# Rearranging the end of the second mixer, and the last token tile's output, in a two-layer trunk kernel

## The chip, the cores and the metric

The kernel runs as one program on one core of a Trainium2 chip. The metric is device time in microseconds. The core has a matmul engine (PE in the profile, with its weight loads shown apart as PEld), three engines that work on tiles (DVE, the vector engine; ACT, the scalar engine; POOL), and queues that issue DMA transfers (most of them from SP). Each engine works through its own list of instructions in order; semaphores make one engine wait for another. Matmul results go to PSUM, of which this program uses eight banks of 128 x 512 floats; everything else lies in SBUF.

## What is computed

The reference is a two-layer encoder over 512 tokens of width 1024. Layer A mixes with a matrix memory, layer B with banded attention; both also attend to 256 memory tokens, and each mixer is followed by a gated MLP with a short convolution. The part that the change touches is layer B's mixer and the final norm:

```python
h = rmsnorm(x, norm_mix_g[l])
proj = h @ b_w_in[bl]
q, q_mem = jnp.split(proj, [B_WIDTH], axis=-1)
mix_out = band_attention(q, k_pad, v_pad, b_rel_bias[bl])      # 12 heads of 64
w_out = b_w_out[bl]
mem_out = memory_attention(q_mem, mem, mem_w_kv[l])            # 4 heads of 64, 256 keys
x = x + jnp.concatenate([mix_out, mem_out], axis=-1) @ w_out
x = x + conv_ffn(rmsnorm(x, norm_ffn_g[l]), ffn_w_up[l], ffn_conv_w[l], ffn_conv_b[l], ffn_w_down[l])
...
return rmsnorm(x, final_g)
```

`k_pad` and `v_pad` are shared keys and values, projected from the normed output of layer A with `w_kv`.

## The kernel before

Activations are kept feature-major: eight tiles of 128 features by 512 tokens. Every matmul operand is split into a high part and a low part in a reduced float type (`split`, L139: the high part is a cast on ACT, L140, the low part a subtraction on DVE, L141). A product is then three matmuls: high by high, high by low, low by high (`mm3`, L192; the PE rows of L194, L195 and L196). A weight tile that arrives by DMA as `wr` becomes `wh` and `wl` in the same way; there are three buffers of `wr` and three of each part.

**Pairs.** Heads are worked on two at a time. The 12 band heads are six pairs, 0 to 5, and the four memory heads are two pairs, 0 and 1. `project_pair(j)` (L1309) makes values, keys and queries of band pair j: three projections of 24 matmuls each, the values transposed (L1323), the queries formed by `queries` and `head_queries` (two casts at L525 and two at L528 on ACT, two subtractions at L526 on DVE, two memsets on POOL at L524). `b_memory_queries(hp)` (L1391) is one projection of 24 matmuls and the same forming of queries. A projection's result is scaled on DVE at L574 (queries) or L1312 (values and keys); only when that has run does its PSUM bank come free.

**Attention.** `memory_attention` (L582) has, for each of two halves of the tokens and each head: scores on PE (L544), a maximum on DVE (L598), the exponential on ACT (L601, twice), a reciprocal (L602) and a scaling (L604, twice) on DVE, four transposes on PE (L613), and a split of the transposed tile (`pt`; ACT L140, DVE L141). Two groups of four matmuls (L627), one for each head, then multiply by the values; `values` (L559) adds their halves (ACT L563, DVE L564). `band_attention` (L1333) does the same by four token tiles T = 0 to 3 of growing width: scores (L544), bias and minimum on DVE (L1350), exponential on ACT (L1354), reciprocal and scaling on DVE (L1355, L1356), transposes (L1365), split, and the products with the values (L1386, L1387).

**PSUM.** The eight banks form three rings: three banks for projections (`mm`, shown as `pmm`), three for scores (`sc`, `psc`), two for transposes and value products (`tr`, `ptr`). A new tile of a ring waits until the last reader of the tile that used the bank before has finished.

**Order.** In this stage nothing is ordered by hand, except that a few instructions are pinned. The code is written as generators that yield after each small piece of PE work. `weave(job, filler, each, lead)` (L225) runs an attention as `job` and takes `each` pieces of the filler for every piece of the job; `chain` puts generators one after another; `until` runs the filler until a result is there; `run` runs it to its end. The filler holds work that depends on little: the remaining projections, then the output projection (`OutProjection.part(g, *ks)`, which loads rows k of `b_w_out` and adds their product into the open sums of output group g). A scheduler of the language then lists the instructions engine by engine, by readiness as it reckons it, so the engines' lists follow the written order only roughly. `reload_x` (L437) issues eight loads on SP that bring the residual back into the buffers `fh` and `fl`, which until then hold the values of band pairs 1 to 4.

**The end.** After the last MLP the output is token-major: four tiles T of 128 tokens, each in two halves of 512 features (`xt[T][0]` and `xt[T][1]`). `add_squares` (L1434) collects sums of squares in pieces, and `final_norm` (L1445) forms the reciprocal root (a square root on ACT, a reciprocal and one Newton step on DVE), scales one half on ACT and the other on DVE, and sends both out by DMA, one from ACT's queue and one from SP's.

Of the kernel before, what the change touches and what calls it, by code (L numbers as in the profile page):

```python
# [12 lines left out]
AF = mybir.ActivationFunctionType  # L13
# [3 lines left out]
P = 128  # L17
D = 1024
# [36 lines left out]
def trunk(  # L55
# [526 lines left out]
    def memory_attention(q, kv, hp, mixes):  # L582
# [40 lines left out]
        for h in range(2):  # L623
            o2 = ps("tr")
            outs.append(o2)
            for i, (a, p) in enumerate(((0, pth), (0, ptl), (1, pth), (1, ptl))):
                nc.tensor.matmul(o2, vs[a][:, 2 * hp + h, :], p[h][:, a, :], start=i == 0, stop=i == 3)  # L627
            yield
# [767 lines left out]
    fill = chain(*(project_pair(j) for j in range(5)), b_memory_queries(0), project_pair(5), b_memory_queries(1))  # L1396
# [7 lines left out]
    until(lambda: 4 in qkv, fill)  # L1404
    weave(band_attention(4, *qkv.pop(4)), fill, 3.456)
    run(fill)
    reload_x()
    fill = chain(outp.part(0, 0, 1), outp.part(0, 2, 6), outp.part(0, 3, 4))
    weave(memory_attention(memq[1], memkv, 1, mixes), fill, 0.48, 4)
    job = band_attention(5, *qkv.pop(5))  # L1410
    fill = chain(fill, outp.part(0, 7))
    weave(islice(job, 8), fill, 2.372)
# [21 lines left out]
    def add_squares(T, t):  # L1434

        if len(sums[T]) == 1:
            V.tensor_scalar(sums[T][0], sums[T][0], 1.0 / D, EPS, op0=ALU.mult, op1=ALU.add)
        elif sums[T]:
            last = sums[T].pop()
            V.scalar_tensor_tensor(sums[T][0], last, 1.0 / D, sums[T][0], op0=ALU.mult, op1=ALU.add)  # L1440
        sums[T].append(small(1))
        sq = sb("t", [P, S])
        A.activation(sq[:, : t.shape[-1]], t, AF.Square, accum_out=sums[T][-1])

    def final_norm(T):  # L1445
        v, r, t = small(1), small(1), small(1)
        first, second = sums[T]
        A.activation(r, second, AF.Sqrt, scale=1.0 / D, bias=first)
        V.scalar_tensor_tensor(v, second, 1.0 / D, first, op0=ALU.mult, op1=ALU.add)
        V.reciprocal(r, r)  # L1450
        V.tensor_mul(t, r, r)
        V.scalar_tensor_tensor(t, t, -0.5, v, op0=ALU.mult, op1=ALU.mult)
        V.scalar_tensor_tensor(r, t, 1.5, r, op0=ALU.add, op1=ALU.mult)
        A.activation(xt[T][0], xt[T][0], AF.Copy, scale=r)
        nc.scalar.dma_start(out[T * P : (T + 1) * P, :S], xt[T][0])
        V.scalar_tensor_tensor(xt[T][1], xt[T][1], r, fgb[1], op0=ALU.mult, op1=ALU.mult)
        nc.sync.dma_start(out[T * P : (T + 1) * P, S:], xt[T][1])
# [80 lines left out]
```

## Time and profile before

| what | value |
|---|---|
| time, median of 3 runs | 1179.51 us (1179.32 to 1180.14) |
| the profiled execution's own time | 1181.13 us |
| its span, first to last instruction | 1179.4 us |
| PE busy over the span | 1167.9 us (99%) |
| DVE, ACT, POOL busy | 941.3, 730.0, 129.7 us |
| mean granted clock of PE | 0.999 |
| second mixer's memory pair 0, first scores to band pair 4 | about 743 to 755 us of the span |
| its end, products of band pair 5 | about 802 us |
| last matmul of the program | issued at 1172.11 us |

The profile gives for each instruction its engine, source line, tiles and shape, its start from the beginning of the span, its duration, and, in brackets, how long the engine had been idle and which instruction released it. Durations of one engine can overlap: matmuls of the same kind follow each other at a shorter distance than each lasts, so for what a matmul costs the distance between starts counts. A line with `x4` is four equal instructions merged. "The windows" are a view that gives, for stretches of the span, how long each engine was busy in them.

### The profile page before, as it was taken

Reading aid. Unit: us, or ns where it says so; the run is one execution under the profiler, and the core shown is the slowest. Engines: PE = TensorE matmul, PEld = TensorE weight load, DVE = VectorE, ACT = ScalarE, POOL = GpSimd, SP = SyncE. Lnnn points to the kernel's source line nnn. Section 1 sums busy time; section 2 is a strip of 40 time slices with the busy share of each in tenths; the row PEclk is TensorE's granted clock in tenths of the full one; section 3 lists DMA queues with packets and bytes.
Section 4 is the critical chain, followed back from the end, with each engine's and each line's share of the span. In section 5 each row is a group of like instructions: output and inputs, shape, how many; then the busy total and the mean of one; then the engine's idle time right before and its main releaser. Section 6 shows DMA issues by size and latency. Waiting matters only on the chain.

```text
span 1179.4 us, 18657 instructions
## 1 busy us (share of the span) xinstructions
PE 1167.9 (99%) x7007; PEld 1033.9 (88%) x7007; DVE 941.3 (80%) x1688; ACT 730.0 (62%) x1294; POOL 129.7 (11%) x222
## 2 busy tenths in 40 slices
PE   8999999999999999999999999999999999999997
PEld 8988888888889999999888888888889999999986
DVE  5877778787979877777697888897897887777755
ACT  5638578654656665556576667776565665666545
POOL 0211101000011111111021000101001011110100
PEclk9999999999999999999999999999999999999999
DMA  8645425244366866666564312335426466566551
GB/s 283 206 116 132 105 54 152 66 136 134 90 155 146 189 157 171 151 154 136 146 196 134 90 54 80 105 104 179 143 90 152 109 137 143 142 143 143 126 161 72
DMA packets 200156, 158.64 MB, mean 135 GB/s; under 512 B 8344, under 2 KB 179838, under 8 KB 200066
## 3 DMA queue, kind: packets, MB, share of 16 engines
q1 hardware_dynamic: 183906, 119.74, 34.7%
q0 software_dynamic: 15584, 36.67, 15.7%
q8 instruction: 55, 0.90, 0.3%
q10 hardware_dynamic: 576, 1.05, 0.2%
q14 instruction: 35, 0.29, 0.1%
HBM read 128.89 MB, written 32.46 MB: 137 GB/s over the span
## 4 chain that ended last, share of the span: by engine, by line
PE 93%; DVE 3%; DMA 2%; ACT 1%; SPq 1%; issue 0%; POOL 0%; POOLq 0%; ACTq 0%; DVEq 0%
PE pmm L194 18%; PE pmm L195 18%; PE pmm L196 18%; PE ptr L195 6%; PE ptr L194 6%; PE ptr L196 6%; PE psc L196 5%; PE psc L195 5%; PE psc L194 5%; PE psc L544 2%; PE ptr L1365 1%; DMA wr<-in_mem_w_kv_dram 1%; PE ptr L1386 1%; PE ptr L1387 1%; DMA u<-in_mem_dram 1%; PE ptr L627 1%
## 5 line engine op out<-in xcount | busy, mean ns | idle before, releaser
L194 PE MATMUL pmm<-u,wh 128*128 128x512 f32 (+1 forms) x968 | 333.0, 344 | 0.2 <-ACT u L140 0.2
L196 PE MATMUL pmm<-u,wl 128*128 128x512 f32 (+1 forms) x968 | 330.7, 342 | 0.0
L195 PE MATMUL pmm<-u,wh 128*128 128x512 f32 (+1 forms) x968 | 330.4, 342 | 0.0
L141 DVE TENSOR_TENSOR wl<-wr,wh 128x1024 fp32r<-128x1024 f32 (+3 forms) x172 | 199.9, 1163 | 81.6 <-ACT wh L140 81.2
L140 ACT CAST wh<-wr 128x1024 fp32r<-128x1024 f32 (+3 forms) x172 | 171.9, 1001 | 93.3 <-PE pmm L195 40.3
L196 PEld LDWEIGHTS pmm<-u,wl 128*128 128x128 f32 x968 | 181.9, 188 | 20.7
L194 PEld LDWEIGHTS pmm<-u,wh 128*128 128x128 f32 x968 | 181.8, 188 | 18.8 <-ACT u L140 1.1
L195 PEld LDWEIGHTS pmm<-u,wh 128*128 128x128 f32 x968 | 182.0, 188 | 18.4 <-DVE u L141 0.5
L194 PE MATMUL ptr<-u,wh 128*128 128x512 f32 x272 | 106.4, 391 | 0.0
L195 PE MATMUL ptr<-u,wh 128*128 128x512 f32 x272 | 106.2, 390 | 0.0
L196 PE MATMUL ptr<-u,wl 128*128 128x512 f32 x272 | 105.8, 389 | 0.0
L778 POOL DMA_DIRECT2D xspill<-t x64 | 55.5, 867 | 432.6 <-ACT t L777 420.1
L834 ACT COPY t<-pmm 128x256 f32<-128x256 f32 x102 | 38.2, 374 | 76.6 <-PE pmm L196 76.5
L141 DVE TENSOR_TENSOR u<-t,u 128x512 fp32r<-128x512 f32 (+1 forms) x94 | 54.3, 604 | 35.4 <-ACT u L140 35.4
L194 PE MATMUL pmm<-u,fh 128*128 128x256 f32 x272 | 75.4, 277 | 0.0
L195 PE MATMUL pmm<-u,fh 128*128 128x256 f32 x272 | 75.2, 277 | 0.0
L196 PE MATMUL psc<-u,wl 128*128 128x256 f32 (+1 forms) x232 | 75.1, 324 | 0.0
L196 PE MATMUL pmm<-u,fl 128*128 128x256 f32 x272 | 75.1, 276 | 0.0
L195 PE MATMUL psc<-u,wh 128*128 128x256 f32 (+1 forms) x232 | 75.1, 324 | 0.0
L194 PE MATMUL psc<-u,wh 128*128 128x256 f32 (+1 forms) x232 | 74.9, 324 | 0.0
L141 DVE TENSOR_TENSOR fl<-pt,fh 128x512 fp32r<-128x512 f32 x102 | 70.3, 689 | 5.1 <-ACT fh L140 1.4
L140 ACT CAST fh<-pt 128x512 fp32r<-128x512 f32 x102 | 62.9, 616 | 8.8 <-DVE pt L888 5.6
(335 smaller groups left out, 2510.4 us busy)
## 6 DMA issues: line engine op xcount, KB each, us to landing
wr<-in_ffn_w_up_dram SPq DMA_DIRECT2D x54, 512.0 KB, 6.5
wr<-in_ffn_w_down_dram SPq DMA_DIRECT2D x38, 512.0 KB, 5.3
pt<-in_ffn_w_up_dram SPq DMA_DIRECT2D x34, 512.0 KB, 8.0
xspill<-t POOLq DMA_DIRECT2D x64, 256.0 KB, 4.5
wr<-in_a_w_in_dram SPq DMA_DIRECT2D x20, 512.0 KB, 3.9
wr<-in_w_kv_dram SPq DMA_DIRECT2D x12, 512.0 KB, 4.1
xspill<-fh POOLq DMA_DIRECT2D x16, 256.0 KB, 2.6
xspill<-fl POOLq DMA_DIRECT2D x16, 256.0 KB, 2.8
```

The source lines that it names most:

```text
L140: high = A.copy(hi, src) if on_act else V.tensor_copy(hi, src)
L141: low = V.tensor_tensor(out=lo, in0=src, in1=f(hi), op=ALU.subtract)
L194: nc.tensor.matmul(o, lh, rh, start=first, stop=False, skip_group_check=more)
L195: nc.tensor.matmul(o, lh, rl, start=False, stop=False, skip_group_check=more)
L196: nc.tensor.matmul(o, ll, rh, start=False, stop=last, skip_group_check=more)
L544: nc.tensor.matmul(o, a, b, start=first and i == 0, stop=i == 1)
L627: nc.tensor.matmul(o2, vs[a][:, 2 * hp + h, :], p[h][:, a, :], start=i == 0, stop=i == 3)
L778: G.dma_start(xspill[j], t, accum_op=ALU.add)
L834: A.copy(o, r[:, :H])
L1365: nc.tensor.transpose(tp[:, b * P : (b + 1) * P], es[T, h][:, b * P : (b + 1) * P], ident)
L1386: nc.tensor.matmul(o2[:, s * P :], w, hi_at(pts[h], s, s, TT - s), start=s == 0, stop=False)
L1387: nc.tensor.matmul(o2[:, s * P :], w, lo_at(pts[h], s, s, TT - s), start=False, stop=s == TT - 1)
```

## The change

The diff has five parts.

1. In `memory_attention` the four matmuls of a head at L627 use both high parts of the probabilities before both low parts.
2. In the filler of layer B's mixer the second memory pair's query projection stands ahead of the three projections of band pair 5, instead of behind them.
3. The rates of the weaves are changed: 1.2 for band pair 4 (3.456 before), 0.8 with a lead of 2 for memory pair 1 (0.48 with a lead of 4), 1.125 for the first part of band pair 5 (2.372). The filler isn't run to its end after band pair 4 any more, so that projections of pair 5 reach into memory pair 1; and `reload_x` is called behind memory pair 1.
4. The Newton step of the final norm is rewritten: with sums scaled by 4/D the root is half of what it was, and one small DVE multiplication goes away.
5. The last token tile (T = 3) is scaled and sent out in two pieces of 256 columns for each half, and the order and queue of the output DMAs change.

```diff
@@ memory_attention
-            for i, (a, p) in enumerate(((0, pth), (0, ptl), (1, pth), (1, ptl))):
+            for i, (a, p) in enumerate(((0, pth), (1, pth), (0, ptl), (1, ptl))):
                 nc.tensor.matmul(o2, vs[a][:, 2 * hp + h, :], p[h][:, a, :], start=i == 0, stop=i == 3)
@@ the second mixer
-    fill = chain(*(project_pair(j) for j in range(5)), b_memory_queries(0), project_pair(5), b_memory_queries(1))
+    fill = chain(*(project_pair(j) for j in range(5)), b_memory_queries(0), b_memory_queries(1), project_pair(5))
     weave(norm.finish(), fill, 1)
...
     weave(memory_attention(memq[0], memkv, 0, mixes), fill, 0.8, 6)
-    until(lambda: 4 in qkv, fill)
-    weave(band_attention(4, *qkv.pop(4)), fill, 3.456)
-    run(fill)
+    until(lambda: 4 in qkv and memq[1] is not None, fill)
+    weave(band_attention(4, *qkv.pop(4)), fill, 1.2)
+    fill = chain(fill, outp.part(0, 0, 1), outp.part(0, 2, 6), outp.part(0, 3, 4))
+    weave(memory_attention(memq[1], memkv, 1, mixes), fill, 0.8, 2)
+    until(lambda: 5 in qkv, fill)
     reload_x()
-    fill = chain(outp.part(0, 0, 1), outp.part(0, 2, 6), outp.part(0, 3, 4))
-    weave(memory_attention(memq[1], memkv, 1, mixes), fill, 0.48, 4)
     job = band_attention(5, *qkv.pop(5))
     fill = chain(fill, outp.part(0, 7))
-    weave(islice(job, 8), fill, 2.372)
+    weave(islice(job, 8), fill, 1.125)
     fill = chain(fill, outp.part(1, 0, 1, 2, 6), outp.part(1, 3, 4, 7))
     weave(job, fill, 1.411)
@@ add_squares
-            V.tensor_scalar(sums[T][0], sums[T][0], 1.0 / D, EPS, op0=ALU.mult, op1=ALU.add)
+            V.tensor_scalar(sums[T][0], sums[T][0], 4.0 / D, 4 * EPS, op0=ALU.mult, op1=ALU.add)
...
-            V.scalar_tensor_tensor(sums[T][0], last, 1.0 / D, sums[T][0], op0=ALU.mult, op1=ALU.add)
+            V.scalar_tensor_tensor(sums[T][0], last, 4.0 / D, sums[T][0], op0=ALU.mult, op1=ALU.add)
@@ final_norm
-        A.activation(r, second, AF.Sqrt, scale=1.0 / D, bias=first)
-        V.scalar_tensor_tensor(v, second, 1.0 / D, first, op0=ALU.mult, op1=ALU.add)
+        A.activation(r, second, AF.Sqrt, scale=4.0 / D, bias=first)
+        V.scalar_tensor_tensor(v, second, -4.0 / D, first, op0=ALU.mult, op1=ALU.subtract)
         V.reciprocal(r, r)
-        V.tensor_mul(t, r, r)
-        V.scalar_tensor_tensor(t, t, -0.5, v, op0=ALU.mult, op1=ALU.mult)
-        V.scalar_tensor_tensor(r, t, 1.5, r, op0=ALU.add, op1=ALU.mult)
-        A.activation(xt[T][0], xt[T][0], AF.Copy, scale=r)
-        nc.scalar.dma_start(out[T * P : (T + 1) * P, :S], xt[T][0])
-        V.scalar_tensor_tensor(xt[T][1], xt[T][1], r, fgb[1], op0=ALU.mult, op1=ALU.mult)
-        nc.sync.dma_start(out[T * P : (T + 1) * P, S:], xt[T][1])
+        V.scalar_tensor_tensor(t, r, v, r, op0=ALU.mult, op1=ALU.mult)
+        V.scalar_tensor_tensor(r, t, 3.0, r, op0=ALU.add, op1=ALU.mult)
+        step = S if T < TT - 1 else MEM
+        for c in range(0, S, step):
+            a, b = (t[:, c : c + step] for t in xt[T])
+            last = c + step == S
+            A.activation(a, a, AF.Copy, scale=r)
+            V.scalar_tensor_tensor(b, b, r, fgb[1][:, c : c + step], op0=ALU.mult, op1=ALU.mult)
+            nc.sync.dma_start(out[T * P : (T + 1) * P, S + c : S + c + step], b)
+            (nc.scalar if last else nc.sync).dma_start(out[T * P : (T + 1) * P, c : c + step], a)
```

Since a scheduler makes the engines' lists, three places show what the second and third part become in them. A row is a line, an operation, the tile written, the tiles read and the shape.

ACT, from the softmax of memory pair 0 on. `psc_8077` and `psc_8078` hold the first half's scores of the two heads; a row of L601 with `x2` is their exponential. Before:

```order
L525 ACTIVATE u_8036<-t_8033 64x512
L528 CAST u_8036<-u_8036 64x512
L601 ACTIVATE t_8093,s_8091<-psc_8077,s_8090 128x256 x2
L601 ACTIVATE t_8114,s_8112<-psc_8078,s_8111 128x256 x2
L601 ACTIVATE t_8139,s_8137<-psc_8123,s_8136 128x256 x2
L140 CAST pt_8075<-ptr_8160 128x2x256
L601 ACTIVATE t_8151,s_8149<-psc_8124,s_8148 128x256 x2
L140 CAST pt_8076<-ptr_8170 128x2x256
```

After:

```order
L525 ACTIVATE u_8036<-t_8033 64x512
L528 CAST u_8036<-u_8036 64x512
L601 ACTIVATE t_8093,s_8091<-psc_8077,s_8090 128x256 x2
L525 ACTIVATE u_8101<-t_8099 64x512
L525 ACTIVATE u_8102<-t_8099 64x512
L528 CAST u_8101<-u_8101 64x512
L528 CAST u_8102<-u_8102 64x512
L601 ACTIVATE t_8126,s_8124<-psc_8078,s_8123 128x256 x2
L140 CAST pt_8075<-ptr_8172 128x2x256
L601 ACTIVATE t_8151,s_8149<-psc_8135,s_8148 128x256 x2
L140 CAST pt_8076<-ptr_8182 128x2x256
L601 ACTIVATE t_8163,s_8161<-psc_8136,s_8160 128x256 x2
```

The four casts that form memory pair 1's queries now stand between the exponentials of the two heads.

PE, in the new list, between that softmax and the products of memory pair 0 (`psc_8253`, `psc_8254` and `psc_8276` are scores of band pair 4, tiles T = 0 and 1; `pmm_8391` is a projection of band pair 5; the L613 rows are memory pair 0's transposes):

```order
L544 MATMUL psc_8254<-u_7885,u_7991 128x128
L544 MATMUL psc_8254<-u_7885,u_7993 128x128
L544 MATMUL psc_8276<-u_7884,u_7990 128x256
L544 MATMUL psc_8276<-u_7884,u_7992 128x256
L613 MATMUL ptr_8192<-ident,t_8151 128x128 x4
L1323 MATMUL pmm_8374<-ident,t_8214 128x128 x3
L613 MATMUL ptr_8199<-ident,t_8163 128x128 x4
L1323 MATMUL pmm_8374<-ident,t_8214 128x128
L194 MATMUL pmm_8391<-u_6428,wh_8387 128x512
L627 MATMUL ptr_8209<-pt_8075,u_7979 128x512
```

Before, eight matmuls of a projection stood between the last two groups of transposes here, and band pair 4's second tile came only after the products.

DVE, at the start of band pair 5 (the L564 rows finish memory pair 1; `psc_8662` and `psc_8663` are the scores of T = 0 for the two heads, `psc_8665` and `psc_8666` after the change). Before:

```order
L564 TENSOR_TENSOR t_8643<-ptr_8630,t_8644 64x512
L1350 ISA t_8668,s_8669<-psc_8662,bias_8658 128x128
L1350 ISA s_8669 128x1
L1350 ISA t_8675,s_8676<-psc_8663,bias_8660 128x128
L1350 ISA s_8676 128x1
L1355 RECIPROCAL s_8670<-s_8670 128x1
```

After:

```order
L564 TENSOR_TENSOR t_8630<-ptr_8614,t_8631 64x512
L1350 ISA t_8671,s_8672<-psc_8665,bias_8661 128x128
L1350 ISA s_8672 128x1
L564 TENSOR_TENSOR t_8630<-ptr_8622,t_8631 64x512
L141 TENSOR_TENSOR wl_8897<-wr_8892,wh_8896 128x768
L141 TENSOR_TENSOR u_8637<-t_8630,u_8636 128x512
L1355 RECIPROCAL s_8673<-s_8673 128x1
L1350 ISA t_8678,s_8679<-psc_8666,bias_8663 128x128
```

Three full-width instructions now stand between the two heads of the first token tile.

## The prediction, before the run

> **What bounds the kernel now.** I read the page, then the windows over the stretch that the change moves, then each engine's rows there.
>
> ```profile
> span 1179.4 us, 18657 instructions
> ...
> PE 1167.9 (99%) x7007; PEld 1033.9 (88%) x7007; DVE 941.3 (80%) x1688; ACT 730.0 (62%) x1294; POOL 129.7 (11%) x222
> ...
> PE 93%; DVE 3%; DMA 2%; ACT 1%; SPq 1%; issue 0%; POOL 0%; POOLq 0%; ACTq 0%; DVEq 0%
> ```
>
> PE is the bound: no matmul is removed, so all that can be won or lost is PE's idle time. A busy share hides it, since matmuls overlap; I price PE by distances between starts.
>
> ```profile
> 751.93 0.40 PE L195 MATMUL pmm<-u,wh 128*128 128x512 f32 x1
> 752.16 0.39 PE L196 MATMUL pmm<-u,wl 128*128 128x512 f32 x1
> ...
> 771.51 1.12 PE L544 MATMUL psc<-u,u 128*128 128x256 f32 x8
> 772.47 0.40 PE L194 MATMUL pmm<-u,wh 128*128 128x512 f32 x1
> ...
> 774.58 0.60 PE L1365 MATMUL ptr<-ident,t 128*128 128x128 f32 x4
> 774.93 0.48 PE L196 MATMUL pmm<-u,wl 128*128 128x512 f32 x1
> ```
>
> So a 512-column matmul takes 0.227 us of PE (0.23 here), a 256-column one 0.96/8 = 0.12, a transpose 0.35/4 = 0.0875; a 128-column score I put at 0.07, by its width. Now the stage, cut at the first scores of memory pair 0, the second head's products (L627), the products of band pair 4, those of memory pair 1, the first matmul of output group 1, and the products of band pair 5:
>
> ```profile
> 743.58:755.48 11.90, 11.72 (x70) 9.40 (x69) 11.69 (x28) 9.97 (x27) 4.03 (x8) 1.00 0.39 122
> 755.48:775.95 20.47, 20.38 (x107) 16.92 (x107) 19.57 (x55) 16.11 (x38) 1.30 (x2) 1.00 0.27 78
> 775.95:786.56 10.61, 10.29 (x61) 8.37 (x59) 8.88 (x23) 8.23 (x24) 0.00 (x0) 1.00 0.48 148
> 786.56:797.03 10.47, 10.47 (x54) 8.47 (x54) 9.57 (x33) 7.81 (x23) 0.00 (x0) 1.00 0.11 29
> 797.03:802.04 5.01, 5.01 (x31) 4.04 (x29) 4.71 (x14) 3.10 (x8) 0.00 (x0) 1.00 0.26 78
> ```
>
> Each row gives length, then busy time of PE, PEld, DVE and ACT. With PE's list priced as above the five stretches need 10.29, 19.32, 8.80, 10.13 and 4.58 us; they take 11.90, 20.47, 10.61, 10.47 and 5.01. So 1.61, 1.15, 1.81, 0.34 and 0.43 us are lost, 5.34 in all, part of it about 0.09 at each change from transposes to matmuls (above, 774.93 lasts 0.48, not 0.39). In the first stretch DVE is busy for 11.69 of 11.90 us: there PE waits for DVE.
>
> **The change, part by part.** *Products at L627.*
>
> ```profile
> 743.58 0.38 PE L544 MATMUL psc<-u,u 128*128 128x256 f32 x1
> ...
> 754.85 0.45 PE L194 MATMUL pmm<-u,wh 128*128 128x512 f32 x1
> 755.48 1.20 PE L627 MATMUL ptr<-pt,u 128*128 128x512 f32 x4 [0.18 <-DVE pt L141]
> ```
>
> The wait stands ahead of the group, not inside it. Its bank is one of two in the `tr` ring, free only when DVE's low split has read the transposes: the same instruction that makes the low part. Taking high parts first can't start the group earlier. I take 0; what it hides behind is that bank, and if DVE were ahead there would be nothing to win either.
>
> *Memory pair 0.* In the new list PE has, between first scores and second L627 group, 19 projection matmuls instead of 24, 18 and 4 score matmuls, 20 transposes and 4 products: 4.31 + 2.16 + 0.27 + 1.75 + 0.91 = 9.40 us, 0.89 less cover than before. The other engines:
>
> ```profile
> 743.51 1.40 DVE L526 SCALAR_TENSOR_TENSOR u<-t,u 64x512 fp32r<-64x512 f32 x2
> 744.97 0.69 DVE L598 TENSOR_REDUCE s<-psc 128x2 f32<-128x512 f32 x1
> ...
> 753.30 1.40 DVE L535 TENSOR_TENSOR u<-t,u 64x512 fp32r<-64x512 f32 x2
> ...
> 756.81 0.94 DVE L141 TENSOR_TENSOR wl<-wr,wh 128x768 fp32r<-128x768 f32 x1
> ...
> 742.24 0.63 ACT L525 ACTIVATE u<-t 64x512 fp32r<-64x512 f32 x1
> 742.90 0.62 ACT L528 CAST u<-u 64x512 fp32r<-64x512 f32 x1
> ...
> 745.69 0.47 ACT L601 ACTIVATE t<-psc,s 128x256 f32<-128x256 f32 x1 [0.87 <-DVE s L598]
> ...
> 749.04 0.59 ACT L140 CAST pt<-ptr 128x512 fp32r<-128x512 f32 x1
> ...
> 760.19 0.84 ACT L140 CAST wh<-wr 128x768 fp32r<-128x768 f32 x1
> ```
>
> DVE's list from L598 to the last `pt` trades two L535 for two L526 (1.40 each way) and gains one 768-wide `wl`, 0.87 by distance. It took 755.48 - 744.97 = 10.51 with no gap; so 11.4 now. ACT's list is longer by four casts between the two heads' exponentials, 0.65 each from start to start. Behind these casts queue the second head's exponential, on it DVE's scaling, PE's transposes, and band pair 4's scores, which want the banks. From L598: 0.72 to the first exponential, four pairs of them at 0.94, four casts 2.60, two `pt` casts at 0.53, one `wh` 0.76, a `pt` cast 0.53, then DVE's split 0.60, `wl` 0.87, split 0.69: 11.6 (durations less the 0.07 or so by which neighbours overlap). I take 11.7. L598 starts 1.39 us after the first scores (744.97 - 743.58), behind the same query casts as now. Together 13.1 against 9.4 of work: 3.7 lost instead of 1.6, **+2.1**. Lower bound +1.1: L598 at once when its scores are there (0.7 after the first, not 1.39), DVE without a gap. Upper +3.0: an estimate, ACT and DVE waiting for each other by 0.2 in each of the four head halves.
>
> *Band pair 4.* From second L627 to L1386 PE has 14.1 us of work instead of 19.3, DVE 13.3 by the same listing, near the share it has now (19.57 of 20.47). The loss of 1.15 is mostly the changes of kind, about ten of them in either list: **0**, from -0.7 to +0.7.
>
> *Memory pair 1.* PE's own work grows from 8.80 to 12.44, since the output projection's matmuls now lie around it; the forming of band pair 5's queries (four casts 2.60, two L526 1.40) comes between its exponentials. Walked as above from L1386: ACT has band pair 4's two copies and the first three exponentials behind it at 4.65; then a cast 0.55, half a pair 0.47, the four casts 2.6, the other half 0.47 and a pair 0.94, two `pt` 1.06, two weight casts 1.5, a `pt` 0.53: 12.8. DVE's 1024-wide `wl` ends at 13.35, its split at 13.95, and the first L627 has its bank at 14.0: 1.56 lost instead of 1.81: **-0.25**, from -1.3 (only changes of kind left) to +1.5 (as in pair 0).
>
> *Band pair 5.*
>
> ```profile
> 788.65 1.09 PE L627 MATMUL ptr<-pt,u 128*128 128x512 f32 x4
> ...
> 788.95 0.27 DVE L1350 CUSTOM_DVE_ANT_0 t<-psc,bias 128x128 f32<-128x128 f32 x1
> ...
> 789.16 0.28 DVE L1350 CUSTOM_DVE_ANT_0 t<-psc,bias 128x128 f32<-128x128 f32 x1
> ...
> 790.71 0.68 DVE L564 TENSOR_TENSOR t<-ptr,t 64x512 f32<-64x512 f32 x1
> ```
>
> Now both heads' T = 0 scores are read before that L564; in the new list the second head's stands behind it, a 768-wide `wl` and a 512-wide split. T = 2's scores take that bank in the `sc` ring. From the second L627 group DVE reads it at 2.06 (790.71 - 788.65) + 0.60 + 0.87 + 0.60 + 0.35 = 4.5; PE comes there after 4 products, 9 projection matmuls and 2 scores, 3.2. A wait of 1.3, less the 0.34 lost now: **+1.0**, from 0 (L564 earlier by the ACT work that now precedes it) to +1.6.
>
> *Queues.* On SP the output weights now go ahead of three residual loads, and two weight DMAs of group 1 behind five loads that wait for band pair 4's values.
>
> ```profile
> fl<-xspill SPq DMA_DIRECT2D x4, 256.0 KB, 4.9
> ...
> wr<-in_b_w_out_dram SPq DMA_DIRECT2D x8, 128.0 KB, 3.1
> ```
>
> Issue of the five (0.4 each) and landing, 3.1 more: about 10 us after L1386, while by PE's list their product comes some 28 us after it. Nothing; uncovered, one load's 5. POOL's memsets for the moved queries go ahead of band pair 4's two bias loads; all of memory pair 0's softmax lies over these. Nothing; uncovered, a load of 256 KB.
>
> *The end.*
>
> ```profile
> 1172.11 0.28 PE L196 MATMUL pmm<-wh,u 128*128 128x256 f32 x1
> ...
> 1174.14 0.16 DVE L1452 SCALAR_TENSOR_TENSOR s<-s,s 128x1 f32<-128x1 f32 x1
> 1174.34 0.16 DVE L1453 SCALAR_TENSOR_TENSOR s<-s,s 128x1 f32<-128x1 f32 x1
> 1174.53 0.75 DVE L1456 SCALAR_TENSOR_TENSOR u<-u,s,bias 128x512 f32<-128x512 f32 x1
> 1175.28 0.37 ACTq L1455 DMA_DIRECT2D out_dram<-u  x1
> ...
> DMA  0000000000049999889999989400000000000000
> ...
> q10 hardware_dynamic: 144, 0.26, 17.1%
> ...
> q1 hardware_dynamic: 567, 0.52, 54.0%
> ```
>
> The strip is 1175 to 1179 in tenths of a microsecond: data moves from 1176.1 to 1177.6. One small multiplication less is 0.19. A 256-column piece takes about 0.50, so the first DMA goes at 1174.86 instead of 1175.3; four issues from two queues end later, at about 1176.0, yet each moves half as much. The first queue row (1175 to 1179) gives 17.1% x 4 us x 16 / 144 = 76 ns a packet, 85 for the 2 KB ones; the second (765.4 to 768.6, weight rows of 1 KB) 54.0% x 3.2 x 16 / 567 = 49, 54 without the small ones. So 512 half packets need 1.8 us where 256 needed 1.4: from 1175.7 to 1177.5, or 1177.0 if they don't queue. **-0.3**; bounds -0.65 and, with 1 KB at the price of 2 KB, +0.9.
>
> [...]
>
> Sum: 2.1 + 0 - 0.25 + 1.0 - 0.3 = +2.55. The profiled execution, 1179.4 of span and 1.7 around it, would go from 1181.13 to 1183.7; it lies 1.62 above the median of the runs, so the median goes from 1179.51 to 1182.1.
>
> **The rivals.** *The waits go away.* Memory pair 0 now comes behind one more projection, 24 x 0.227 = 5.4 us in which DVE and ACT have little to do; both arrive with empty queues, L598 starts at once, and even spreading leaves only the changes of kind: 1.6 and 1.8 become about 0.7 and 0.5. That is -2.2, with the end -2.5: 1177.0; half of it, 1178.3. For it: DVE's 11.69 of 11.90 shows a backlog that DVE could have worked off. Against it: the cover beside the chain is shorter, the chain longer. It decides if the second L627 group starts less than 11 us after the first scores.
>
> *Nothing but the end.* The scheduler listed all by readiness, so pair 0's loss may be made good in pair 1 and band pair 5, whose PE work has grown: -0.3 to +0.9, 1179.2 to 1180.4. For it: 3.64 us more projection work in memory pair 1. Against it: the bank wait of band pair 5, which is behind it.
>
> **How the numbers follow.** 0.2% is 2.4 us, about what a measurement can tell from no change. The order costs waits, total +1.2 to +4.5: 0.66, of which 0.54 lie above 2.4. The waits go away: 0.18, half beyond -2.4. Nothing but the end: 0.16. So faster 0.09, same 0.37, slower 0.54. The time is 1182.1; its own range 1180.7 to 1184.0. For 8 in 10 the low end goes to 1178.7, into the rivals, the high one to 1184.4 (pair 0 and band pair 5 at their upper bounds, and a little of pair 1).
>
> **What would show it.** In the new trace: first scores of memory pair 0 to second L627 in about 13 us, with DVE and ACT both close to full; L627 waiting for DVE ahead of each group and never inside it; T = 2's scores of band pair 5 idle for DVE about 1.3 us after some 3 us of work; no weight late in the output projection; the time from last matmul to end shorter by about 0.3. I am wrong if the first is under 12 us, or if memory pair 1 falls well below 14 from L1386 to L627.

## The result, and the profile after

The changed kernel takes 1185.34 us (median of 6 runs, 1184.83 to 1188.98), the kernel before 1179.41 us beside it (6 runs, 1178.96 to 1180.14): a ratio of 1.0052, with a 95% interval of 1.0042 to 1.0063. Slower was the forecast, but by 2.6 us; it is 5.9, and 1185.34 lies above the range.

The page of the changed kernel shows more busy time of PE, though not one matmul was added:

```profile
span 1183.9 us, 18657 instructions
...
PE 1171.8 (99%) x7007; PEld 1035.6 (87%) x7007; DVE 941.7 (80%) x1685; ACT 730.7 (62%) x1295; POOL 129.2 (11%) x222
...
PE 95%; ACT 2%; DVE 2%; issue 0%; POOL 0%; ACTq 0%; POOLq 0%; DVEq 0%
```

PE was busy for 1167.9 us before and is now for 1171.8. The same 7007 matmuls count as 3.9 us more, so the 99% says nothing; the distances between starts do. Followed along the program, the n-th matmul of the changed kernel starts 1.57 us earlier than that of the kernel before until the second mixer's end begins (the profiled execution of the kernel before had lost some 1.7 us in its first 45), and 4.84 us later from the products of band pair 5 to the last matmul, without a further step between. So 6.41 us are lost in the mixer's end, and the rest of the program but the tail runs as before.

The windows, cut at the same marks as in the prediction (first scores of memory pair 0, second L627 group, products of band pair 4, first L627 of memory pair 1, products of band pair 5), with PE, PEld, DVE, ACT and POOL busy in that order, then the granted clock:

```profile
747.39:762.28 14.89, 13.02 (x65) 10.53 (x66) 12.16 (x27) 10.95 (x28) 4.00 (x8) 0.89 0.33 99
762.28:777.75 15.47, 15.36 (x84) 12.27 (x82) 14.16 (x48) 11.57 (x32) 1.09 (x2) 1.00 0.19 55
777.75:792.28 14.53, 14.25 (x77) 11.25 (x77) 13.98 (x30) 11.77 (x30) 0.00 (x0) 1.00 0.41 131
792.28:807.53 15.25, 14.15 (x71) 10.82 (x71) 13.18 (x45) 10.20 (x29) 0.00 (x0) 1.00 0.16 46
...
747.39:807.53 60.14, 56.78 (x293) 44.88 (x294) 53.48 (x148) 44.49 (x117) 5.09 (x10) 0.97 0.27 82
```

and the whole stretch in the kernel before:

```profile
743.58:802.04 58.46, 57.87 (x315) 47.21 (x314) 54.43 (x150) 45.22 (x118) 5.33 (x10) 1.00 0.30 91
```

With PE's list priced as in the prediction (0.227 us for 512 columns, 0.12 for 256, 0.0875 for a transpose), what is lost is length less work:

| stretch | lost before | forecast | lost after |
|---|---|---|---|
| memory pair 0 | 1.62 | 3.7 | 5.50 |
| band pair 4 | 1.14 | 1.15 | 1.37 |
| memory pair 1 | 1.81 | 1.56 | 2.09 |
| band pair 5 | 0.76 | 1.8 | 2.58 |
| from first scores to products of band pair 5 | 5.33 | 8.2 | 11.55 |

Three things are to be read here. First, PE's work in the whole stretch is 48.6 us now and was 53.1, while DVE's is nearly the same, 53.48 and 54.43: DVE has 4.9 us more to do there than PE, where before the two were nearly even (1.3). So DVE is now the more loaded engine of this stretch, though it is idle for 6.7 of the 60.14 us as well: of the 6.2 us that are lost more, this difference can explain 3.6 (an estimate, 4.9 less 1.3). Second, the first row has a granted clock of 0.89. Third, every stretch loses more, memory pair 0 most.

Where the 4.5 us of work went is shown by the chain of waits just ahead of the first scores (start, duration, work):

```profile
745.79 0.24 PE pmm L196
746.06 0.64 ACT u L525
746.73 0.62 ACT u L528
747.37 0.64 ACT u L525
748.03 0.69 DVE u L526
748.75 0.70 DVE s L598
```

and by the timeline of DVE, ACT and PE there:

```profile
735.88 0.69 DVE L574 SCALAR_TENSOR_TENSOR t<-pmm,rb 128x512 f32<-128x512 f32 x1
...
739.71 1.05 ACT L140 CAST wh<-wr 128x1024 fp32r<-128x1024 f32 x1 [3.16 <-PE pmm L195]
745.15 0.84 ACT L140 CAST wh<-wr 128x768 fp32r<-128x768 f32 x1 [4.38 <-DMA wr<-in_b_w_out_dram]
746.06 0.63 ACT L525 ACTIVATE u<-t 64x512 fp32r<-64x512 f32 x1
...
747.39 0.39 PE L544 MATMUL psc<-u,u 128*128 128x256 f32 x1
```

and, in the kernel before, by the same scaling and the cast ahead of the queries:

```profile
737.45 0.69 DVE L574 SCALAR_TENSOR_TENSOR t<-pmm,rb 128x512 f32<-128x512 f32 x1
...
741.29 1.05 ACT L140 CAST wh<-wr 128x1024 fp32r<-128x1024 f32 x1 [3.16 <-PE pmm L195]
```

Memory pair 0's queries are scaled (L574) by 736.57, and their first cast (L525) starts at 746.06, 9.5 us later; before it was 4.1 (738.14 to 742.24, from the same two instructions). The chain has PE's L196 ahead of that cast. That matmul belongs to the second projection of band pair 5, which is the last reader of the normed activations that keys and values are made of. The program has 50 buffers of the kind `u`; the semaphore that the cast waits for is raised by that matmul, since its destination is the buffer of an activation tile: it can be written only when this projection has read it. The change puts a projection of 24 matmuls ahead of band pair 5's; the release, the casts and the scores all came that much later in PE's list. Meanwhile ACT stood idle for 3.16 and then 4.38 us, and PE did projection work beside which the others had little to do: from 742.05 to the first scores at 747.39 PE was busy for 5.33 us, DVE for 1.37 and ACT for 2.12.

The drop of the clock, in windows of 3.41 us from the middle of memory pair 0, and PE's rows there:

```profile
754.40:757.82 3.42, 1.97 (x13) 1.42 (x12) 3.42 (x10) 3.21 (x11) 0.66 (x2) 1.00 0.50 153
757.82:761.23 3.41, 3.37 (x13) 2.97 (x13) 2.87 (x6) 1.18 (x2) 0.00 (x0) 0.50 0.00 1
```

```profile
754.03 0.44 PE L544 MATMUL psc<-u,u 128*128 128x128 f32 x2 [0.37 <-ACT t L601]
...
756.98 0.51 PE L544 MATMUL psc<-u,u 128*128 128x256 f32 x2 [1.12 <-ACT t L601]
...
758.67 1.06 PE L613 MATMUL ptr<-ident,t 128*128 128x128 f32 x4
...
760.17 1.58 PE L627 MATMUL ptr<-pt,u 128*128 128x512 f32 x4
```

PE first waits for banks that the exponentials (ACT L601) still read; then, from 757.82 to 761.23, the granted clock is 0.50: four transposes last 1.06 us instead of 0.60, and the first L627 group 1.58 us instead of 1.20.

In band pair 5 the wait stands elsewhere than forecast:

```profile
794.94 0.69 DVE L564 TENSOR_TENSOR t<-ptr,t 64x512 f32<-64x512 f32 x1
...
795.73 0.61 ACT L140 CAST u<-t 128x512 fp32r<-128x512 f32 x1
...
795.02 0.45 PE L544 MATMUL psc<-u,u 128*128 128x256 f32 x2
796.40 0.96 PE L194 MATMUL pmm<-u,wh 128*128 128x512 f32 x3 [0.93 <-ACT u L140]
```

PE has come to the product of memory pair 1's values with the output weights while these values are still being added (L564) and cast. The row has 0.93 us of idle time; by the distance between starts the wait costs 1.10.

The end:

```profile
1176.95 0.28 PE L196 MATMUL pmm<-wh,u 128*128 128x256 f32 x1
...
1179.24 0.88 DVE L1458 SCALAR_TENSOR_TENSOR u<-u,s,bias 128x256 f32<-128x256 f32 x2
1180.17 0.36 ACTq L1460 DMA_DIRECT2D out_dram<-u  x1
1180.21 0.38 SPq L1460 DMA_DIRECT2D out_dram<-u  x1
1180.69 0.41 SPq L1459 DMA_DIRECT2D out_dram<-u  x1
```

From the last matmul to the end of the span it is 6.98 us (1183.93 - 1176.95); it was 7.30 (1179.41 - 1172.11). From the residual add on DVE to the scaling it is 1.97 us instead of 2.10, which is the shorter Newton step, and from the scaling to the end 4.69 instead of 4.88, which is the output in two pieces with its other order of DMAs.

### The profile page after: what moved, and what is told of

Same layout as the page of the kernel before. It is cut to its first block, busy times and chain, and to the rows that moved or that the text cites. A ratio compares the mean times of both kernels' runs of the same rounds, so it can differ in the third digit from the quotient of the medians.

```text
span 1183.9 us, 18657 instructions
## 1 busy us (share of the span) xinstructions
PE 1171.8 (99%) x7007; PEld 1035.6 (87%) x7007; DVE 941.7 (80%) x1685; ACT 730.7 (62%) x1295; POOL 129.2 (11%) x222
## 4 chain that ended last, share of the span: by engine, by line
PE 95%; ACT 2%; DVE 2%; issue 0%; POOL 0%; ACTq 0%; POOLq 0%; DVEq 0%
PE pmm L194 18%; PE pmm L195 18%; PE pmm L196 18%; PE ptr L195 6%; PE ptr L194 6%; PE ptr L196 6%; PE psc L194 5%; PE psc L196 5%; PE psc L195 5%; PE psc L544 2%; PE ptr L1365 1%; PE ptr L1386 1%; PE ptr L1387 1%; PE ptr L627 1%; PE ptr L613 0%; ACT t L601 0%
## 5 line engine op out<-in xcount | busy, mean ns | idle before, releaser
L196 PE MATMUL pmm<-u,wl 128*128 128x512 f32 (+1 forms) x968 | 330.8, 342 | 0.0
L195 PE MATMUL pmm<-u,wh 128*128 128x512 f32 (+1 forms) x968 | 330.3, 341 | 0.1
L196 PEld LDWEIGHTS pmm<-u,wl 128*128 128x128 f32 x968 | 181.8, 188 | 20.9 <-DVE wl L141 0.2
L195 PEld LDWEIGHTS pmm<-u,wh 128*128 128x128 f32 x968 | 182.0, 188 | 19.2 <-DVE u L141 1.0
L195 PE MATMUL ptr<-u,wh 128*128 128x512 f32 x272 | 106.2, 391 | 0.0
L196 PE MATMUL ptr<-u,wl 128*128 128x512 f32 x272 | 105.8, 389 | 0.0
L195 PE MATMUL pmm<-u,fh 128*128 128x256 f32 x272 | 75.2, 277 | 0.0
L195 PE MATMUL psc<-u,wh 128*128 128x256 f32 (+1 forms) x232 | 75.2, 324 | 0.0
L196 PE MATMUL psc<-u,wl 128*128 128x256 f32 (+1 forms) x232 | 75.1, 324 | 0.0
L196 PE MATMUL pmm<-u,fl 128*128 128x256 f32 x272 | 75.1, 276 | 0.0
```

The lines of the kernel that those rows point to most:

```text
L195: nc.tensor.matmul(o, lh, rl, start=False, stop=False, skip_group_check=more)
L196: nc.tensor.matmul(o, ll, rh, start=False, stop=last, skip_group_check=more)
```

## The experiments

Times are medians; the kernel before was run beside each. "D" in the expectations is the theory that memory pair 0's queries wait for buffers.

**The end alone** (the kernel before with the fourth and fifth part of the diff).

> The kernel before with the fourth and fifth part of the change alone (shorter Newton step, last tile in two pieces); mixer and L627 as before. Theory 'the end is worth what the prediction said': from the last residual add on DVE to the end of the span 6.6 us instead of 7.0, median 0.2 to 0.5 us below the kernel before. [...] Rival 'the rest of the change hides a loss at the end': equal or up to 0.9 above. In the mixer nothing: about 5.9 us lost there as in the kernel before.

1179.44 us (11 runs) against 1179.27 (17 runs), ratio 1.0001 (0.9993 to 1.0010). In its trace the time from the last matmul to the end is 7.00 us, 0.30 less than before, and it is 6.98 to 7.01 in all ten further traces that have this end. So the step is there at the size forecast. In the medians the spread of the runs, 3 us, hides 0.3.

**The casts behind band pair 4.**

```diff
-        memq[hp] = queries((yield from project(b_w_in, AW + hp * P, act)), norm.row)
+        o = yield from project(b_w_in, AW + hp * P, act)
+        if hp == 0:
+            memq[hp] = queries(o, norm.row)
+            return
+        q = sb("t", [P, S])
+        V.scalar_tensor_tensor(q, o, HD**-0.5, norm.row, op0=ALU.mult, op1=ALU.mult)
+        memq[hp] = q
...
-    weave(memory_attention(memq[1], memkv, 1, mixes), fill, 0.8, 2)
+    weave(memory_attention(head_queries(memq[1]), memkv, 1, mixes), fill, 0.8, 2)
```

> The changed kernel, but the forming of memory pair 1's queries (four casts on ACT, two subtractions on DVE) is written behind band pair 4; the projection and its scaling stay where they are. Theory A (the casts between the exponentials delay the scores' banks, and PE's waits there cut the granted clock): first scores of memory pair 0 to second L627 group in 10.5 to 11.5 us instead of 14.88, no stretch at half clock, and the median 3 to 4 us below the changed kernel, about 1181.5 to 1182.3. Rival B (the shorter cover, not the casts): the stretch stays above 13.5 us and the median falls by less than 1. Rival C (the casts cost as much where they now stand): the stretch falls to 11, but band pair 4 or memory pair 1 lose 2 or more, so the median falls by 1 to 2.

1186.45 us against 1179.27: 7.2 us more, where the changed kernel has 6.0 (below). Windows of memory pair 0 and of memory pair 1 in this run:

```profile
747.24:759.21 11.97, 11.58 (x69) 9.40 (x69) 11.00 (x25) 8.56 (x24) 4.04 (x8) 1.00 0.32 100
...
774.89:793.85 18.96, 17.01 (x92) 13.27 (x92) 16.33 (x33) 14.79 (x35) 0.00 (x0) 1.00 0.33 108
```

Memory pair 0 did become short, 11.97 instead of 14.89 us, at a granted clock of 1.00, with 1.9 us lost instead of 5.5. But band pair 4 lost 3.48 instead of 1.37 and memory pair 1 4.40 instead of 2.09, so all was given back: 12.45 us over the stretch, against 11.55. The casts between the exponentials are a real wait, yet moving them wins nothing here, where the stretch holds less work for PE than for DVE. Rival C came nearest, and even it was too hopeful.

**Memory pair 0's values in place of memory pair 1's.**

```diff
-    mm3(self.o[j], wh[:, i, c], wl[:, i, c], *self.mixes[k], self.n[g] == 1, self.n[g] == KT)
+    mix = self.mixes[6 if (j0, k, self.w.name) == (0, 7, b_w_out.name) else k]
+    mm3(self.o[j], wh[:, i, c], wl[:, i, c], *mix, self.n[g] == 1, self.n[g] == KT)
```

> The changed kernel, but the last rows of output group 0 (nine matmuls) multiply memory pair 0's values, long there, instead of memory pair 1's: the output is not the reference's. PE's list keeps its order there. Theory A (PE stands 1.1 to 1.4 us at this product, because memory pair 1's values are just being added and split): the wait of 1.10 us at 795.2 us goes away. Step of the prediction (the bank of the third token tile's scores waits for DVE anyway): about 0.4 us of it is left at those scores, so the median falls by 0.7 to 1.0. Rival (DVE's list is the bound, the bank wait takes all of it): the median falls by less than 0.3.

1185.06 us against 1179.27. The 1.10 us at this product are gone, and PE loses the same time at the next scores, which wait for DVE; the first of these waits:

```profile
796.99 0.62 PE L544 MATMUL psc<-u,u 128*128 128x384 f32 x2 [0.24 <-DVE s L1351]
```

(L1351 is L1350 in the other kernels.) From the second L627 group to the first matmul of output group 1 it lost 2.03 us, the changed kernel 2.04. The rival holds: PE waits for DVE there in any case, and the product only happened to stand first in PE's list.

**The old order at L627** (the first part of the diff undone).

> The changed kernel with the old order of the four matmuls at L627. Theory A (0, as predicted; the first group took 1.42 us instead of 0.98 because the clock was at half there): median within 0.3 us of the changed kernel. Rival (changing between two stationary operands costs 0.1 us a matmul): 16 groups of two more changes, 0.4 to 1.5 us faster than the changed kernel.

1184.17 us against 1179.27. This is 1.1 less than the changed kernel's distance, as the rival has it, but not for the rival's reason: at a granted clock of 1.00 the L627 groups of memory pair 1 take, by starts, 0.91 and 0.92 us in the new order (the changed kernel) and 0.93 in the old (the kernel before), and there are 8 groups, not 16. In the trace of this run the granted clock is 1.00 over memory pair 0 (748.23 to 761.87), which takes 13.64 us instead of 14.89. Why four of the five runs have a mean clock of 0.998 or 0.999, against two of eleven of the changed kernel, was not found.

**The changed kernel again.**

> The changed kernel unchanged, on the same chip and beside the same runs of the kernel before as the next three. About 5.5 to 6.5 us above the kernel before. Runs with a mean granted clock of 0.999 should lie about 1.2 us below those with 0.997, if a stretch of 3.41 us at half clock in memory pair 0 is what tells them apart.

1185.36 us (5 runs) against 1179.37: 6.0 more, and a trace with the same stretch at a granted clock of 0.50 (757.97 to 761.38). Of the 11 runs of the changed kernel in both comparisons, eight have a mean clock of 0.997 (median 1185.5), two 0.999 (1184.92 and 1184.76), one 0.995 (1188.98). So about 0.7 us instead of the 1.2 expected, from two runs only; what made the one run 3.5 us slower still is open.

**The order of the filler alone** (the kernel before with one line).

```diff
-    fill = chain(*(project_pair(j) for j in range(5)), b_memory_queries(0), project_pair(5), b_memory_queries(1))
+    fill = chain(*(project_pair(j) for j in range(5)), b_memory_queries(0), b_memory_queries(1), project_pair(5))
```

> The kernel before with one line of the second part alone: the second memory pair's queries ahead of band pair 5's projections; old rates, old L627, old end. Theory D (memory pair 0's query casts can't write before PE has read the activations for keys and values in pair 5's second projection, whose buffers they take; the moved projection puts that 24 matmuls later, and 5.2 us of PE work are gone from beside the attentions, 47.9 instead of 53.1): 47.9 us of PE work from first scores to the products of band pair 5, 4 to 7 us more lost than in the kernel before, median 4 to 7 above it. Rival E (the new rates are the cost, the order alone is harmless): within 2 us of the kernel before.

1187.00 us against 1179.37, 7.6 more. The whole loss comes with this one line, and the rest of the change takes 1.6 of it back, 0.3 of that at the end. PE's work from first scores to the products of band pair 5 is 49.3 us (in the changed kernel 48.6; the 47.9 of the expectation was added up too low), and 12.6 us are lost.

**Other buffers, in the changed kernel.**

```diff
-    def head_queries(t, scale=1.0):
-        qs, ls = ([sb("u", [P, S], F32R) for _ in range(2)] for _ in range(2))
+    def head_queries(t, scale=1.0, tags="uu"):
+        qs, ls = ([sb(tag, [P, S], F32R) for _ in range(2)] for tag in tags)
...
-        memq[hp] = queries((yield from project(b_w_in, AW + hp * P, act)), norm.row)
+        memq[hp] = queries((yield from project(b_w_in, AW + hp * P, act)), norm.row, ("uu", ("fh", "fl"))[hp == 0])
```

> The changed kernel, with memory pair 0's four query tiles in the buffers of fh and fl, which then stand empty, instead of u. Theory D: the query casts follow their scaling within 2 us (now 9.5), the first scores come some 30 matmuls earlier, PE's work from them to the products of band pair 5 rises from 47.9 us to 54 or more, the loss in the mixer falls from 12.3 to 8 or less, and the median to 1178.5 to 1181. Rival E (rates and the casts between the exponentials are the cost, wherever the stretch starts): the loss falls by less than 2 and the median stays above 1183.

1180.10 us (11 runs) against 1179.37, ratio 1.0007 (0.9998 to 1.0016): 5.3 us of the 6.0 are gone. DVE's scaling, ACT's casts, PE's first scores, and the windows' row for the whole stretch:

```profile
736.99 0.69 DVE L574 SCALAR_TENSOR_TENSOR t<-pmm,rb 128x512 f32<-128x512 f32 x1
...
737.72 1.29 ACT L525 ACTIVATE fh<-t 64x512 fp32r<-64x512 f32 x2
...
740.17 0.28 PE L544 MATMUL psc<-u,fh 128*128 128x256 f32 x1
...
740.17:800.88 60.71, 59.40 (x322) 48.51 (x320) 55.25 (x149) 45.08 (x118) 5.33 (x10) 1.00 0.35 107
```

The casts start 0.04 us after the scaling ends, the first scores come 36 matmuls earlier in PE's list, PE has 54.7 us of work in the stretch beside DVE's 55.25, and 6.0 us are lost instead of 11.55. The four tiles no longer take buffers of `u`, so that later tiles get other ones too; that memory pair 0's wait is the only one which went away with them isn't shown.

**Other buffers, in the kernel before** (the same edit, with the changed end).

> The kernel before with the same other buffers for memory pair 0's queries, and with the changed end. Theory D: the same wait stands in the kernel before (scaled at 738.1 us, cast at 742.2), so its first scores come 15 or more matmuls earlier, the loss in its mixer falls from 5.9 us by 1 to 3, and the median lies 1 to 3 us below the kernel before. Rival (what is lost there is mostly changes between transposes and matmuls, which more cover can't win back): within 0.7 us of the kernel before.

1178.39 us against 1179.37, ratio 0.9992 (0.9984 to 1.0001): 1.0 us lower, the least that was expected, of which the end makes 0.3, and not to be told from no change. 4.85 us are lost in the stretch instead of 5.33: there, more cover has little left to win.

**Other buffers, with the order of the filler alone** (the one line, the buffers, the changed end).

> The kernel before, with the one line of the query order (as in the run of the order alone), memory pair 0's queries in the buffers of fh and fl, and the changed end. Theory D: what made the order alone cost 7.6 us was the wait for buffers, so it falls away: 1178 to 1180.5. Rival (the order costs by itself, since less projection work is left for band pair 4 and memory pair 1): above 1182.

1178.55 us (11 runs, 1178.37 to 1178.86) against 1179.41, ratio 0.9991 (0.9982 to 1.0000). With free buffers the order that had cost 7.6 us costs nothing: with the same buffers and end, but the old order, it was 1178.39. Beside the run above with the new rates, 1180.10, it also shows what the rates are worth (with L627 and the place of the residual loads): they cost about 1.5 us once the buffers are free, where in the buffers of `u` the full change lies 1.6 below the order alone.

**Useless work in the waits.**

```diff
-            ss = [ps("sc")[:, :n] for _ in range(2)]
-            scores(ss, q, slice(T * P, n), k, slice(0, n))
+            full = [ps("sc") for _ in range(2)]
+            ss = [o[:, :n] for o in full]
+            for h in range(2):
+                for _ in range((1, 2)[h] if (j, T) == (4, 0) else 0):
+                    head_scores(full[h], h, q, slice(T * P, n), k, slice(0, S), True)
+                head_scores(ss[h], h, q, slice(T * P, n), k, slice(0, n), True)
```

> The changed kernel with six matmuls of 512 columns more, 1.36 us of PE, whose result is written over: they repeat the first token tile's scores of band pair 4 (two ahead of the first head's, four ahead of the second's), where PE waited 0.35 and 1.28 us for the banks of the next scores. The clock falls to half for one window of 3.41 us behind a window in which PE was busy for 1.69 to 2.08 us (four traces), and did not where it was busy for 2.27 or more. Theory (the waits close the clock gate, and that costs about 1.2 us in four runs of five): with the useless work every window there holds more than 2.3 us, no run has a clock of 0.997, first scores to second L627 falls from 14.9 to 13.4 to 13.9 us, and the median is 0.5 to 1.3 us below the changed kernel, about 1184.1 to 1184.9, though PE does more. Rival (the clock falls for another reason, or costs nothing because PE waits for DVE there anyway): equal to the changed kernel or up to 1.4 slower.

1184.22 us against 1179.41, which is 1.1 to 1.2 less than the changed kernel's distance, though PE does 1.36 us more; the clock of its five runs is 0.998 or 0.999. Memory pair 0, and the 3.41 us of its filled waits:

```profile
747.11:760.75 13.64, 13.01 (x72) 10.22 (x72) 12.05 (x27) 10.93 (x28) 3.99 (x8) 1.00 0.32 93
754.12:757.53 3.41, 3.23 (x20) 2.48 (x18) 3.41 (x11) 3.19 (x11) 0.63 (x2) 1.00 0.51 154
```

13.64 us, the same as in the run with the old L627, whose clock is 1.00 there too. So 1.25 of the 14.89 us go with the fall of the clock (an estimate, 14.89 less 13.64). With the waits filled the clock stayed up in all five runs, as the theory has it; with the old order of L627 it did in four of five without any filling. So the runs fit the theory but don't decide it: they show the granted clock, not what lowers it.

**The weight cast behind the queries** (the cast of the first output weights, which stands on ACT just ahead of the query casts, is queued behind them; `after_queries` is set where the output weights are loaded; the lines that keep the last query cast in `behind` are left out here).

```diff
-        return parts(load(*args))
+        if not (after_queries and behind[0]):
+            return parts(load(*args))
+        raw = load(*args)
+        with tc.issue_after(behind[0]):
+            return parts(raw)
```

> The changed kernel, with the cast of the first output weights (768 columns, at 745.15 us on ACT, just ahead of memory pair 0's query casts) queued behind those query casts; buffers as in the changed kernel. Theory D (the casts wait for buffers that PE's first L196 of pair 5's second projection frees, which ends at 746.02; the first cast starts at 746.06): the casts start no earlier than that, the first scores move by less than 0.5 us, and the median is within 1 us of the changed kernel. Rival (the weight cast, which waits on ACT for the moved projection to end, is what holds the queries up): the casts start before 742 us, the scores some 4 us earlier, and the median falls by 2 us or more.

1187.41 us against 1179.66. With the weight cast out of the way, ACT's row says what the casts wait for (L533 and L202 here are L525 and L196):

```profile
739.20 1.05 ACT L140 CAST wh<-wr 128x1024 fp32r<-128x1024 f32 x1 [3.17 <-PE pmm L201]
745.54 0.63 ACT L533 ACTIVATE u<-t 64x512 fp32r<-64x512 f32 x1 [5.29 <-PE pmm L202]
...
817.21 0.50 PE L201 MATMUL pmm<-u,wh 128*128 128x512 f32 x1 [1.53 <-DVE u L141]
```

5.29 us for PE's L196, as theory D has it; the first scores come at the same place of PE's list. The total was to stay within 1 us of the changed kernel and is 1.8 above it. All four runs have a clock of 0.996 or 0.997, but that is not where the 1.8 us lie: at the products of band pair 5 the trace of this run is 0.27 us ahead of the changed kernel's (807.26 against 807.53). They are lost behind these, in the last row, where PE waits 1.53 us in the output projection for the low part of band pair 5's values. In both traces DVE has that split behind an instruction (L888 of the changed kernel) that waits for a DMA; it starts at 815.86 here and at 814.23 in the changed kernel, whose PE has no wait there. Why the DMA comes later is open.

## Why the prediction went wrong, point by point

**What bounds the kernel.** No matmul was removed, and PE's lost time alone decided, as said: 6.41 us lost in the mixer less 0.3 won at the end are 6.1, near the median's 5.9. Not all of it is idle time, though: an estimated 1.25 us go with the fall of the clock. But the claim that PE is the bound was taken from the page for the whole program. For this stretch it stops being true with the change: DVE has 53.48 us to do there, PE 48.6.

**Memory pair 0, +2.1, measured +3.9.** This term is above its upper bound of +3.0. The direction was right, and so was the chain from the casts over the exponentials to the banks of band pair 4's scores: PE waits 0.37 and 1.12 us at these scores for ACT's L601, and with the casts moved the pair took 11.97 us. Two of the signs did not come. No L627 group of this pair waits in the trace, ahead of it or inside; and DVE and ACT are busy for 12.16 and 10.95 of 14.89 us, not close to full. The walk gave 13.1 us, and 13.64 were measured in two traces with the clock at 1.00 there, so the walk itself was 0.5 short. The remaining 1.25 us the prediction lacks altogether: it priced PE's waits as idle time and took PE's speed after them as given, without a reason. The mark for being wrong (under 12 us) missed on the other side.

**The cause behind it, not asked.** The prediction took from the new list that PE has five projection matmuls fewer beside memory pair 0, and in the first rival that this pair "now comes behind one more projection". It did not ask why these scores should come 24 matmuls later, which only the one line of the order brought about. The runs show it: a buffer of `u` that band pair 5's second projection frees. With other buffers the order costs nothing (1178.55 against 1187.00). That wait stood already in the profile of before as 4.1 us between L574 and L525, behind a weight cast that hid it.

**Band pair 5, +1.0, measured +1.8.** The wait was forecast at the third token tile's scores, for DVE. In the trace PE stands before that, at the product of memory pair 1's values; taking that wait away put the loss where the prediction had it, at unchanged size. So the mechanism holds and the term was 0.8 too small, above its upper bound of +1.6. The sum priced one bank wait of 1.3 us; in the run with the other values PE loses 2.03 us up to output group 1, in several short waits.

**Memory pair 1, -0.25, measured +0.28, and band pair 4, 0, measured +0.23.** Both inside their bounds. From the products of band pair 4 to the first L627 it took 14.53 us, against 14.0.

**L627 and the queues, 0.** The order of L627 itself costs nothing at a granted clock of 1.00 (0.91 and 0.92 us a group against 0.93). The queues' weights were never waited for in the trace of the changed kernel; the one ACT row that names a DMA (745.15, 4.38 us) is one where the DMA is not what came last: its two transfers had been issued at 734.56 and 734.95, ten microseconds before, the seven transfers of this kind from 734.6 to 747.0 land 2.3 to 3.1 us after their issue, and the buffer of `wh` that it writes was read by the last L195 of band pair 5's first projection until 745.12 (not of the moved one, as the rival in the run of the weight cast has it).

**The end, -0.3, measured -0.3**. The total held. The small multiplication was worth 0.13 instead of 0.19, and the two pieces 0.19.

**The rivals.** "The waits go away" was refuted by its own test: 14.89 us, not under 11. Its argument, that DVE and ACT arrive with empty queues, was true (ACT's 4.38 us idle, above), and is just what made the change slow: they were idle because they could not start. "Nothing but the end" was refuted in memory pair 1 and band pair 5, which gave nothing back.

**The step that failed** is the size of two terms of the sum. Memory pair 0 cost 1.8 us more than its +2.1, 0.5 for the walk and 1.25 for the clock, which the sum put at nothing; band pair 5 cost 0.8 more than its +1.0. With 0.5 more in memory pair 1 and 0.2 in band pair 4 these make up the 3.4 us by which the sum fell short. Behind them lies what the prediction didn't look for: the late release of the buffers. It left 4.5 us of PE's work outside the four stretches, which were then billed one by one; with other buffers PE's work there is 54.7 us and the loss 6.0. That DVE's 53.5 us kept any stretch from winning back what another lost fits with the run of the casts behind band pair 4, but is argued, not tested by itself.

That the kernel would be slower was forecast, and in part this was luck. With free buffers the order costs nothing and the rates 1.5 us; most of the 5.9 us hang on a wait that the prediction does not contain.

## What to carry to other kernels

When a change moves a projection ahead of a chain, find out what starts the chain: not only its operands, but the last reader of the buffers that it writes. Then count, over the whole run of dependent stages and not stage by stage, PE's work against that of the busiest other engine; here, where PE's had become the smaller, two runs that moved waits about won next to nothing, and what helped was more of PE's work beside the chain. Look at the granted clock behind the waits too: here, behind waits of 0.37 and 1.12 us, it was 0.50 for 3.41 us, and memory pair 0 took 14.89 us against 13.64 in two traces with the clock at 1.00.

## What the runs showed of the hardware

In the trace of the changed kernel the granted clock is 0.50 from 757.82 to 761.23, for 3.41 us, and 1.00 in the windows next to it on either side. Five more traces have windows to set beside the one ahead of that fall:

| run | window | PE busy in it | granted clock in it | granted clock behind it |
|---|---|---|---|---|
| changed kernel | 754.40 to 757.82 | 1.97 us | 1.00 | 0.50 to 761.23 |
| changed kernel again | 754.56 to 757.97 | 2.08 us | 1.00 | 0.50 to 761.38 |
| order alone | 755.69 to 759.10 | 2.01 us | 1.00 | 0.88 over memory pair 0 (748.74 to 763.57) |
| old order at L627 | 756.39 to 759.80 | 2.27 us | 1.00 | 1.00 to 761.87 |
| useless matmuls | 754.12 to 757.53 | 3.23 us | 1.00 | 1.00 to 760.95 |
| kernel before, near its start | 6.01 to 9.42 | 2.06 us | 1.00 | 1.00 to 12.83 |

PE's busy time does not settle it: the clock fell behind 2.08 us in one trace and stayed at 1.00 behind 2.06 us in another. With the waits filled PE is busy for 3.23 us of such a window instead of 1.97 and the clock stays at 1.00, which fits the theory; with the old order at L627 it stays there behind 2.27 us without any filling. That the waits of memory pair 0 brought the clock down is the author's reading; it was not shown. The mean clock is 0.999 in two of the 11 runs of the changed kernel and 0.995 or 0.997 in the others; what sets it in a given run is open.
